# A Mamba-2 and attention trunk on one core: weight-pair stores queued behind the next loads, and the output projection in half-precision pairs from the second block on

## The chip, the cores and the metric

One core of one Trainium2 chip runs the whole program in one launch. The metric is the device time of that core in microseconds (us). The engines are PE (matrix products; PEld is its loading of the stationary operand), DVE (vector operations), ACT (scalar functions), POOL, and SP, which here only issues transfers. Each works through its own list of instructions in order and waits on signals of the others.

## The reference, cut to what matters

2048 tokens of width 1024 go through one Mamba-2 layer, then one attention layer, then a normalization. The change lies in the Mamba-2 layer alone:

```
proj = rms_norm(x) @ w_in              # z (2048), xBC (3072), dt (32 heads)
xBC  = silu(causal_conv4(xBC))         # xs (2048), B and C (4 groups x 128)
y    = scan over time of (x, dt, B, C) in chunks, plus D * x
y    = y * silu(z)                     # 4 groups of 512 channels
y    = y * rsqrt(mean(y*y over the group) + eps) * g_out
h    = x + y @ w_out                   # (2048 x 2048) @ (2048 x 1024)
```

All is float32, and the result has to keep more precision than a single product in half precision or in the fast float format (fp32r) gives.

## The kernel before

**Products.** Every large product is made of three (`mm3`, L86 to L88): each operand is a pair of a high part and the remainder (low part), and high x high, high x low and low x high are added up in PSUM. Pairs are either fp32r (`split`: ACT writes the high part, L109 or with a scale L112, DVE the low part, L110 or L113) or half-precision, f16 (`pair16`: ACT L117, DVE L118). f16 has little range, so values in f16 pairs are first multiplied by a power of two (`up`) that is worked out on the chip from a sum of squares (`powers`, with a PE product at L144 that adds over the partitions), and the result is multiplied by the inverse (`down`).

**Tiling.** The Mamba layer goes through 4 blocks b of 512 tokens, and in each through 4 groups g of channels: 16 items (b, g). For each item `ssd(b, g)` runs over 4 chunks c of 128 tokens. Between its steps a loop places pieces of the other work: the output product `outp` of the item before, and the input products `xbc` and `zgate` of the item behind; in the timeline these are what PE does between the short steps of `ssd`. In block 0 the loop also places `scan(g)`, which reads the weights of a later group of w_in and sums their squares (ACT L180) to find the power. A framework schedules: it writes each engine's list from the program's order, with priorities (`high_priority(AHEAD)`, 10 steps, for making and loading weights) and from buffers that come free. Weight pairs live in `wsp` (6 buffers), raw weights in `wraw` (3).

**Weights.** In block 0 `wpair` loads raw weights of w_in, makes an f16 pair of two k steps (L117, L118) and stores it to DRAM (`wi_d`, L209); later blocks load that pair (L211). For the output product, block 0 loads w_out, multiplies it by g_out and makes an fp32r pair (`wunit`, L130, L112, L113), and stores its two halves (`wo_d`, L511, 64 stores of 256 KB). Blocks 1 to 3 load each pair back (L506, 96 loads of 512 KB).

**The end of a chunk in `ssd`.** y is multiplied by the gate and `down` on DVE (L678). ACT sums its squares into `ms` (L680). PE transposes y in four pieces (L683), ACT and DVE make an fp32r pair of it (L685, tile yT), and `outp` uses it as the stationary operand against wsp (group `mm<-wsp,yT` in the profile). The factor 1/rms per token (`rr`, L690) is applied when the product is added to the residual hs (L519). The list of DVE also holds, for the next chunk, the differences L634 on the tile big, which comes by a transfer from cumT (L622); ACT then takes the exponential (L635) and DVE multiplies (L636).

**The start.** Before the first item the power of w_in's group 0 is found in two scans: kind 0 (B and C), then kinds 1 and 2 together (xs and z): four squares of tiles hs and four of tiles yT on ACT, L144 on PE, the powers on DVE, and with them the first weight pairs. Then `steps(0)` makes the step sizes (L533 on PE, 16 products, and L573), and `xbc(0,0)`, `zgate(0,0)` run together with the scan of group 1 (tiles hx).

## Time and profile before

| | |
|---|---|
| median of 3 runs | 3200.43 us (3199.44 to 3203.22) |
| the profiled execution | 3204.34 us, span 3202.6 us |
| granted clock of PE | 0.995 |
| busy PE, DVE, ACT | 96%, 75%, 60% of the span |
| start (before the first item's work) | 0 to 80 us |
| block 0 (with the making of weights) | 80 to 480 us |
| blocks 1 to 3 | 480 to 1460 us, then to 1650 with the start of attention between |
| attention | 1650 to 3202 us |

A row of the timeline has the start in us, the length in us, the engine, the line, what is written and read (tiles by the program's names, then shape and type), and in square brackets how long the engine had been idle and what released it. A row of grouped waits has the engine and line that waited, what for, the total in us, the times and the longest. Lengths of PE products overlap, so the pace is read from start to start.

### The profile page before, as it was taken

What the parts mean: (1) busy time and instruction counts of PE and PEld (TensorE: products, weight loads), DVE (VectorE), ACT (ScalarE), POOL (GpSimd) and SP (SyncE); (2) the same over time, 40 slices, a digit from 0 to 9 for tenths busy, and PEclk for the clock granted to TensorE, in tenths of its full rate; (3) what the DMA queues carried; (4) which work ended last, traced back from release to release, by engine and by line L of the source; (5) the groups of instructions that cost most, each with busy time, mean ns of one, the idle gap of its engine ahead of it and who ended that gap; (6) DMA issues with size and microseconds to landing.
All of it is one profiled execution on the core that took longest, in us unless ns stands there. A gap on an engine that the chain in (4) does not pass through costs nothing.

```text
span 3202.6 us, 51345 instructions
## 1 busy us (share of the span) xinstructions
PE 3085.4 (96%) x17744; PEld 2163.4 (68%) x17744; DVE 2401.2 (75%) x5178; ACT 1914.1 (60%) x4817; POOL 609.1 (19%) x842
## 2 busy tenths in 40 slices
PE   6999999999999999999999999999999999999998
PEld 3455555666655566665878888877777777777777
DVE  7778887767677676767876665678888888888675
ACT  8667554444455444455645554477877778778522
POOL 0212122121122212212111211322212122222100
PEclk9999999999999999999999999999999999999999
DMA  8667645334443345334476656853444434443485
GB/s 285 229 214 230 229 144 194 127 126 145 141 157 130 115 151 189 127 128 142 141 271 218 225 190 194 265 111 78 95 81 84 81 78 96 79 97 99 101 270 159
DMA packets 207113, 497.61 MB, mean 155 GB/s; under 512 B 27746, under 2 KB 51042, under 8 KB 205412
## 3 DMA queue, kind: packets, MB, share of 16 engines
q1 hardware_dynamic: 165444, 370.04, 35.6%
q0 software_dynamic: 41408, 124.29, 15.9%
q8 instruction: 140, 2.29, 0.3%
q14 instruction: 121, 0.99, 0.1%
HBM read 362.22 MB, written 131.99 MB: 154 GB/s over the span
## 4 chain that ended last, share of the span: by engine, by line
PE 64%; DVE 13%; ACT 8%; DMA 8%; issue 6%; POOL 1%; SPq 0%; ACTq 0%; DVEq 0%; POOLq 0%
PE mm L86 13%; PE mm L87 12%; PE mm L88 12%; PE tr L1044 6%; PE tr L87 3%; PE tr L1054 3%; PE tr L1055 3%; PE tr L86 3%; PE tr L88 3%; DVE cacc L460 3%; DMA big<-cumT 2%; DMA wraw<-in_ssm_w_in_dram 1%; DVE big L634 1%; ACT Pr L1029 1%; PE tr L656 1%
## 5 line engine op out<-in xcount | busy, mean ns | idle before, releaser
L118 DVE SCALAR_TENSOR_TENSOR PTs<-tr,PTs 128x512 f16<-128x512 f32 (+3 forms) x640 | 374.9, 607 | 93.9 <-ACT PTs L117 86.8
L117 ACT ACTIVATE PTs<-tr 128x512 f16<-128x512 f32 (+3 forms) x640 | 328.5, 541 | 141.4 <-PE tr L1044 140.3
L1017 DVE TENSOR_REDUCE mx<-mm 128x1 f32<-128x512 f32 (+2 forms) x631 | 375.7, 608 | 45.7 <-PE mm L88 42.6
L1029 ACT ACTIVATE Pr<-mm,nm 128x512 f32<-128x512 f32 (+2 forms) x631 | 395.7, 636 | 23.1 <-DVE nm L1021 21.4
L1044 PE MATMUL tr<-pack,Pr 128*128 128x128 f32 x2176 | 317.6, 273 | 1.0 <-ACT Os L1061 0.9
L86 PE MATMUL mm<-K,xT 96*128 96x512 f32 (+2 forms) x639 | 288.2, 451 | 23.3 <-ACT Pr L1029 21.8
L86 PE MATMUL mm<-xT,wsp 128*128 128x512 f16 (+1 forms) x800 | 304.9, 381 | 0.3 <-DVE sz L484 0.3
L88 PE MATMUL mm<-xT,wsp 128*128 128x512 f16 (+1 forms) x800 | 303.4, 380 | 1.4 <-DVE wsp L118 1.3
L87 PE MATMUL mm<-xT,wsp 128*128 128x512 f16 (+1 forms) x800 | 303.7, 380 | 0.0
L1044 PEld LDWEIGHTS tr<-pack,Pr 128*128 128x128 f32 x2176 | 253.5, 141 | 49.7 <-ACT Os L1061 1.7
L648 ACT ACTIVATE Xw<-tr,d_wend 128x64 f32<-128x64 f32 x512 | 183.4, 359 | 133.3 <-DVE Xd L644 133.3
L460 DVE SCALAR_TENSOR_TENSOR cacc<-craw,pack,cacc 128x512 f32<-128x512 f32 x288 | 213.6, 764 | 30.5 <-ACT cacc L458 28.9
L86 PE MATMUL mm<-wsp,xT 128*128 128x512 f16 (+1 forms) x640 | 232.4, 363 | 1.6 <-ACT craw L454 1.6
L88 PE MATMUL mm<-K,xT 96*128 96x512 f32 (+2 forms) x639 | 231.6, 362 | 0.0
L87 PE MATMUL mm<-wsp,xT 128*128 128x512 f16 (+1 forms) x640 | 231.6, 362 | 0.0
L87 PE MATMUL mm<-K,xT 96*128 96x512 f32 (+2 forms) x639 | 231.4, 362 | 0.0
L88 PE MATMUL mm<-wsp,xT 128*128 128x512 f16 (+1 forms) x640 | 231.1, 362 | 0.0
L1054 PE MATMUL tr<-PTs,xT 128*128 128x512 f16 (+3 forms) x640 | 222.0, 348 | 0.1
L86 PE MATMUL mm<-wsp,yT 128*128 128x512 f32 x512 | 208.1, 409 | 13.3 <-DVE sz L484 4.7
L1055 PE MATMUL tr<-PTs,xT 128*128 128x512 f16 (+3 forms) x640 | 219.4, 347 | 0.0
L606 POOL TENSOR_TENSOR Xp<-Xw,Xp 128x512 fp32r<-128x512 f32 x64 | 81.8, 1278 | 711.3 <-ACT Xp L605 382.4
L88 PE MATMUL mm<-wsp,yT 128*128 128x512 f32 x512 | 203.0, 397 | 1.4 <-DVE yT L110 1.4
(411 smaller groups left out, 7418.2 us busy)
## 6 DMA issues: line engine op xcount, KB each, us to landing
wsp<-wi_d SPq DMA_DIRECT2D x96, 512.0 KB, 3.7
wsp<-wo_d SPq DMA_DIRECT2D x96, 512.0 KB, 3.5
big<-cumT SPq DMA_DIRECT2D x64, 512.0 KB, 4.9
wi_d<-wsp SPq DMA_DIRECT2D x32, 512.0 KB, 3.4
wo_d<-wsp SPq DMA_DIRECT2D x64, 256.0 KB, 2.5
xT<-qn_d POOLq DMA_DIRECT2D x64, 256.0 KB, 4.4
K<-kn_d POOLq DMA_DIRECT2D x15, 1024.0 KB, 9.2
hx<-in_ssm_w_in_dram SPq DMA_DIRECT2D x48, 256.0 KB, 4.3
```

The source lines that it names most:

```text
L86: mm(out, l_hi, r_hi, start=start, stop=False)
L87: mm(out, l_hi, r_lo, start=False, stop=False)
L88: mm(out, l_lo, r_hi, start=False, stop=stop)
L117: self.nc.scalar.activation(hi, src, AF.Copy, scale=scale)
L118: self.nc.vector.scalar_tensor_tensor(lo, src, scale, hi, ALU.mult, ALU.subtract)
L460: nc.vector.scalar_tensor_tensor(acc, raw[:, k:k + TB], wk[k], acc, ALU.mult, ALU.add)
L648: act(Xw[:, hc], px[:, hc], AF.Copy, scale=wend[:, h0 + h:h0 + h + 1])
L1017: v.tensor_reduce(mx[:, n:n + 1], s[:, :w], AX.X, ALU.max)
L1029: nc.scalar.activation(x[:, :w], s[:, :w], AF.Exp, bias=nm, accum_out=sm[:, n:n + 1])
L1044: nc.tensor.transpose(pt[:, j * P:(j + 1) * P], st["P"][j][kb], self.ident)
L1054: nc.tensor.matmul(st["O"][:, c], vals[h][:, kb, :], u[:, 0], start=kb == 0, stop=False)
L1055: nc.tensor.matmul(st["O"][:, c], vals[h][:, kb, :], u[:, 1], start=False, stop=kb == nk - 1)
```

## The change

It has three parts.

1. *Stores of pairs.* `wpair` first issues the loads of both raw tiles of a pair and then converts them; the store of the pair goes into a list `owed` and is issued (`settle`) behind the loads of the next pair.
2. *The start.* The scan of kinds 1 and 2 is two scans: kind 1 before `steps(0)`, kind 2 together with `xbc(0,0)`; the scan of group 1 runs together with `zgate(0,0)` alone.
3. *The output product.* Block 0 works as before, but stores nothing; ACT takes the sum of squares of each of the 32 weight tiles besides. At the end of block 0 a power of two for w_out is worked out (`out_power`). Block 1 loads the raw tiles again, makes f16 pairs of two k steps (the gain is g_out times the power) and stores them, 16 stores of 512 KB. Blocks 2 and 3 load one such pair of 512 KB for two k steps. From block 1 on, y is brought to f16's range per token: three DVE operations on one column turn the sum of squares into a power of two (L740 to L742), ACT multiplies y by it (L743), and then y is transposed (L745) and made into an f16 pair. The inverse power goes into `rr`.

```
+    def settle(self):
+        for d, u in self.owed:
+            self.nc.sync.dma_start(d, u)
+        self.owed = []
...
             if b == 0:
+                raws = []
                 for j in range(2):
...
+                    raws.append(raw)
+                self.settle()
+                for j, raw in enumerate(raws):
                     self.pair16(u[:, j, 0], u[:, j, 1], raw, self.up[:, g, kind:kind + 1])
-                nc.sync.dma_start(d, u)
+                self.owed.append((d, u))
             else:
+                self.settle()
                 nc.sync.dma_start(u, d)
...
-        rest = self.scan(0, (1, 2), lambda kind: first.pop(0), True)
+        rest = [self.scan(0, (kind,), lambda kind: first.pop(0), True) for kind in (1, 2)]
...
-        for part in (hold, self.prep(0, self.g0), rest, self.steps(0), together(self.xbc(0, 0), ahead),
+        for part in (hold, self.prep(0, self.g0), rest[0], self.steps(0), together(self.xbc(0, 0), rest[1]),
                      together(self.zgate(0, 0), ahead)):
...
+    def w_out(self, b, g, n, j, made):
...
+        with self.tc.high_priority(AHEAD):
+            if b == 0:
+                raw, u = self.raw(False), self.t(self.wp, "wsp", [P, 2, TB], F32R, bufs=WSP)
+                load(raw, j)
+                self.settle()
+                self.split(u[:, 0], u[:, 1], raw, gain(self.go, j))
+                at = 8 * g + 4 * n + j
+                nc.scalar.activation(self.t(self.sp, "yt", [P, D], BF16, bufs=2)[:, :TB], raw, AF.Square,
+                                     scale=gain(self.go, j), accum_out=self.wss[:, at:at + 1])
+                return u[:, 0], u[:, 1]
+            u, d = self.t(self.wp, "wsp", [P, 2, 2, TB], F16, bufs=WSP), self.wo_d[g, n, j // 2]
+            if b == 1:
+                raws = [self.raw(False) for _ in range(2)]
+                for i in range(2):
+                    load(raws[i], j + i)
+                self.settle()
+                for i in range(2):
+                    self.pair16(u[:, i, 0], u[:, i, 1], raws[i], gain(self.gou, j + i))
+                self.owed.append((d, u))
+            else:
+                self.settle()
+                nc.sync.dma_start(u, d)
+        made[j + 1] = u[:, 1, 0], u[:, 1, 1]
+        return u[:, 0, 0], u[:, 0, 1]
+
+    def out_power(self):
...
+        v.tensor_reduce(ss, self.wss, AX.X, ALU.add)
+        self.powers(ss, 1, up, self.wod)
+        v.tensor_scalar(self.gou, self.go, up, None, ALU.mult)
...
     def outp(self, b, g):
...
-                if b:
-                    with self.tc.high_priority(AHEAD):
-                        u = self.t(self.wp, "wsp", [P, 2, TB], F32R, bufs=WSP)
-                        nc.sync.dma_start(u.bitcast(F32), d)
-                    return [u[:, i, :] for i in range(2)]
-                w = self.wunit(a["ssm_w_out"][r0:r0 + P, n * 512:(n + 1) * 512], 512,
-                               self.go[:, 4 * g + j:4 * g + j + 1])
-                for i in range(2):
-                    nc.sync.dma_start(d[:, i], w[i].bitcast(F32))
-                return w
+                return self.w_out(b, g, n, j, made)
...
     def ssd(self, b, g):
...
             act(junk, y, AF.Square, scale=0.5 * 512.0 ** -0.5, accum_out=ms[:, c:c + 1])
+            if b:
+                e = self.t(self.sm, "pwe", [P, 1], I32)
+                v.tensor_scalar(e, ms[:, c:c + 1].bitcast(I32), 24, None, ALU.logical_shift_right)
+                v.tensor_scalar(e, e, -1, 127 + 63 + 8, ALU.mult, ALU.add)
+                v.tensor_scalar(pw[:, c:c + 1].bitcast(I32), e, 23, None, ALU.logical_shift_left)
+                act(y, y, AF.Copy, scale=pw[:, c:c + 1])
...
-            u = self.t(self.sp, "yT", [P, 2, 4, P], F32R, bufs=4)
-            self.split(u[:, 0], u[:, 1], ps.rearrange("p (j t) -> p j t", j=4))
+            u = self.t(self.sp, "yT", [P, 2, 4, P], F16 if b else F32R, bufs=4)
+            (self.pair16 if b else self.split)(u[:, 0], u[:, 1], ps.rearrange("p (j t) -> p j t", j=4))
...
-        v.tensor_scalar(rr, r, 0.5, None, ALU.mult)
+        if b:
+            v.tensor_scalar(pw.bitcast(I32), pw.bitcast(I32), -1, 0x7F000000, ALU.mult, ALU.add)
+            v.scalar_tensor_tensor(rr, r, self.wod, pw, ALU.mult, ALU.mult)
+        else:
+            v.tensor_scalar(rr, r, 0.5, None, ALU.mult)
```

Since the framework writes the lists, these are the places at which they differ most. In the new program the lines have moved: L678 is L734, L680 is L736, L683 is L745, L674 is L730, L673 is L729, L634 is L690, L605 is L661, L460 is L473, L622 is L678, L206 is L213, L519 is L572, L533 is L588; L196 is the store in `settle`, L511 the raw load of w_out.

The list of SP, block 0, where the first output product's weights are made; wraw are raw weights, wsp pairs, wi_d and wo_d the places in DRAM. Before:

```order
L206 DMA wraw_1577<-in_ssm_w_in_dram 128x512
L622 DMA big_1659<-cumT_424 128x1024
L209 DMA wi_d<-wsp_1510 128x2048
L130 DMA wraw_1842<-in_ssm_w_out_dram 128x512
L209 DMA wi_d<-wsp_1572 128x2048
L130 DMA wraw_1852<-in_ssm_w_out_dram 128x512
L130 DMA wraw_1901<-in_ssm_w_out_dram 128x512
L511 DMA wo_d<-wsp_1844 128x512
L511 DMA wo_d<-wsp_1854 128x512
L511 DMA wo_d<-wsp_1844 128x512
L130 DMA wraw_1911<-in_ssm_w_out_dram 128x512
```

The same place now:

```order
L213 DMA wraw_1593<-in_ssm_w_in_dram 128x512
L196 DMA wi_d<-wsp_1528 128x2048
L511 DMA wraw_1860<-in_ssm_w_out_dram 128x512
L511 DMA wraw_1871<-in_ssm_w_out_dram 128x512
L196 DMA wi_d<-wsp_1590 128x2048
L678 DMA big_1889<-cumT_409 128x1024
L175 DMA hx_1705<-in_ssm_w_in_dram 128x512 x2
L511 DMA wraw_1921<-in_ssm_w_out_dram 128x512
```

The stores of w_out pairs are gone from between the raw loads; stores of w_in pairs (wi_d) stand where they stood, one pair behind the loads.

The list of DVE behind y in the second chunk of item (1,1); st is the state, cacc the convolution. Before:

```order
L678 SCALAR_TENSOR_TENSOR y_6277<-y_6277,down,sz_5936 128x512
L674 TENSOR_TENSOR st_373_2063<-st_373_2063,tr_6344 128x512
L634 TENSOR_SCALAR big_6678<-big_6678,d_cum_4090 128x128 x7
L673 TENSOR_TENSOR st_373_2063<-st_373_2063,d_dec_4092 128x512
L634 TENSOR_SCALAR big_6678<-big_6678,d_cum_4090 128x128
L110 TENSOR_TENSOR yT_6387<-tr_6382,yT_6387 128x512
```

The same place now:

```order
L734 SCALAR_TENSOR_TENSOR y_6369<-y_6369,down,sz_5992 128x512
L730 TENSOR_TENSOR st_388_2083<-st_388_2083,tr_6436 128x512
L690 TENSOR_SCALAR big_6780<-big_6780,d_cum_4110 128x128
L740 TENSOR_SCALAR pwe_6475<-ms_6089 128x1
L690 TENSOR_SCALAR big_6780<-big_6780,d_cum_4110 128x128
L741 TENSOR_SCALAR pwe_6475<-pwe_6475 128x1
L690 TENSOR_SCALAR big_6780<-big_6780,d_cum_4110 128x128
L742 TENSOR_SCALAR pw_6090<-pwe_6475 128x1
```

The three operations of the power (pwe, pw) stand among the differences L690, the first of which comes ahead of them and needs the tile big from its transfer.

The list of ACT at the start: yt is a scratch tile, hs and yT hold raw weights of kinds 1 and 2. Before:

```order
L180 ACTIVATE yt_322,ss_307<-hs_210 128x1024
L180 ACTIVATE yt_327,ss_307<-yT_211 128x1024
L180 ACTIVATE yt_331,ss_307<-yT_212 128x1024
L180 ACTIVATE yt_335,ss_307<-yT_213 128x1024
L180 ACTIVATE yt_339,ss_307<-yT_214 128x1024
L117 ACTIVATE wsp_428<-big_205,up 128x256
L117 ACTIVATE wsp_461<-big_205,up 128x256 x2
```

The same place now:

```order
L180 ACTIVATE yt_325,ss_310<-hs_213 128x1024
L117 ACTIVATE wsp_413<-big_208,up 128x256
L117 ACTIVATE wsp_439<-big_208,up 128x256 x2
L117 ACTIVATE wsp_465<-big_209,up 128x256 x2
L117 ACTIVATE wsp_499<-big_209,up 128x256 x2
L117 ACTIVATE wsp_545<-hs_210,up 128x512 x2
L592 ACTIVATE yt_360<-tr_342,dtdown 64x512
L180 ACTIVATE yt_427,ss_424<-yT_214 128x1024
```

The squares of kind 2 (yT) have moved behind the weight pairs of B, C and the first of xs, and behind the step sizes.

More of the change, by code (lines that the diff above doesn't have):

```diff
@@ L280, in layer_constants @@
         self.xdown = cp.tile([P, 1], F32, name="xdown")
+        self.wss, self.gou = (cp.tile([P, n], F32, name=m) for m, n in (("wss", 32), ("gou", 16)))
+        self.wod = cp.tile([P, 1], F32, name="wod")
         self.dtdown = cp.tile([P, 1], F32, name="dtdown")
@@ L488, in zgate, with load, gain @@
         self.sz[b, g] = out
+    def w_out(self, b, g, n, j, made):
+        if j in made:
+            return made.pop(j)
+        nc = self.nc
+        def load(raw, j):
+            r0 = g * 512 + j * P
+            nc.sync.dma_start(raw, self.a["ssm_w_out"][r0:r0 + P, n * 512:(n + 1) * 512])
+        def gain(x, j):
+            return x[:, 4 * g + j:4 * g + j + 1]
+        with self.tc.high_priority(AHEAD):
[23 more added lines that the diff above has]
+    def out_power(self):
+        v = self.nc.vector
+        ss = self.t(self.sm, "ss", [P, 3, 4], bufs=2)[:, 0, 0:1]
+        v.tensor_reduce(ss, self.wss, AX.X, ALU.add)
+        up = self.t(self.sm, "up0", [P, 2], bufs=1)[:, 0:1]
+        self.powers(ss, 1, up, self.wod)
+        v.tensor_scalar(self.gou, self.go, up, None, ALU.mult)
+        v.tensor_scalar(self.wod, self.wod, 0.5, None, ALU.mult)
     def outp(self, b, g):
@@ L522, in outp @@
         if g == G - 1:
+            if b == 0:
+                self.out_power()
             for i in range(4):
@@ L595, in ssd @@
         ms = self.t(self.sm, "ms", [P, 4])
+        pw = self.t(self.sm, "pw", [P, 4])
         self.yT[b, g] = []
@@ L1246, in run @@
             self.wi_d = [dp.tile([G, KD // 2, P, 2, 2, n], F16, name=f"wi{i}_d") for i, n in enumerate((256, 512, 512))]
-            self.wo_d = dp.tile([G, 2, 4, P, 2, TB], F32, name="wo_d")
+            self.wo_d = dp.tile([G, 2, 2, P, 2, 2, TB], F16, name="wo_d")
             self.xq = whole.enter_context(tc.tile_pool(name="xq", bufs=8, side="right"))
```

4 lines of the change are left out of this document (2 added, 2 removed).

## The prediction

> **What bounds the kernel now.** I read the page's busy times first, then a table of five stretches of the span, and only then single rows of the stretches that the change touches.
>
> ```profile
> PE 3085.4 (96%) x17744; PEld 2163.4 (68%) x17744; DVE 2401.2 (75%) x5178; ACT 1914.1 (60%) x4817; POOL 609.1 (19%) x842
> 0.00:80.00 80.00, 54.73 (x254) 28.75 (x255) 57.62 (x182) 64.70 (x124) 5.61 (x20) 0.96 0.88 284
> 80.00:480.00 400.00, 374.46 (x2171) 217.17 (x2170) 326.04 (x669) 261.04 (x631) 74.03 (x90) 0.98 0.64 209
> 480.00:1460.00 980.00, 967.48 (x5713) 584.66 (x5712) 700.81 (x1422) 476.90 (x1288) 202.53 (x250) 1.00 0.43 144
> 1460.00:1650.00 190.00, 178.12 (x1049) 136.90 (x1047) 140.88 (x296) 107.02 (x265) 37.06 (x45) 1.00 0.52 171
> 1650.00:3202.50 1552.50, 1510.63 (x8565) 1195.97 (x8564) 1175.81 (x2612) 1004.39 (x2511) 289.90 (x437) 1.00 0.53 140
> ```
>
> In a row of stretches stand its limits, its length, then busy us and instructions of PE, PEld, DVE, ACT and POOL, the clock, the DMA share and GB/s. PE is busy 96% of the span, so time goes only where PE's own work shrinks or one of its few idle stretches closes. The change ends with the Mamba part, near 1650 us; the 1552 us behind it (attention) run the same instructions and I count nothing there. Blocks 1 to 3 (480 to 1460) leave PE idle for 12.5 us of 980: there, a shorter matmul is worth nearly its full size, and any new wait of PE costs nearly its full size. Block 0 (80 to 480) leaves 25.5 us idle, the start 25 us, the end of the Mamba part 12 us. So I go through four places: the output matmuls of blocks 1 to 3, the new step in front of the transposes of y, the start, and block 0 with what moves from it into block 1.
>
> **1. Half-precision output matmuls, blocks 1 to 3.** Two rows of a run of them in float pairs, 22 intervals apart, and two rows of the input projection, whose operands are half-precision, 5 apart:
>
> ```profile
> 855.33 0.40 PE L87 MATMUL mm<-wsp,yT 128*128 128x512 f32 x1
> 860.36 0.39 PE L88 MATMUL mm<-wsp,yT 128*128 128x512 f32 x1
> 903.98 0.38 PE L86 MATMUL mm<-xT,wsp 128*128 128x512 f16 x1
> 905.06 0.38 PE L88 MATMUL mm<-xT,wsp 128*128 128x512 f16 x1
> L86 PE MATMUL mm<-wsp,yT 128*128 128x512 f32 x512 | 208.1, 409 | 13.3 <-DVE sz L484 4.7
> ```
>
> Start to start that is 5.03/22 = 228.6 ns against 1.08/5 = 216 ns, for the same 128x512 product. The durations overlap, so the intervals count. Of each of the three lines 512 run in four blocks, 384 in blocks 1 to 3: 1152 matmuls x 12.6 ns = 14.5 us. Bounds: 13 us if a tenth of them wait for something else anyway; 23 us if the durations (0.40 against 0.38) told the gain rather than the intervals. I take 15. The Trainium skill, TensorE: Matmul & The Clock Gate, section "Wait — 56ns, not 53.3ns?", gives 215.7 ns for 512 columns without a word on the type; the half-precision rows agree, the float rows do not, and by that rule this term would be nothing.
>
> **2. The step between y and its transposes.** In blocks 1 to 3 each of 48 chunks gets three tiny dependent DVE operations and an ACT copy over 128x512 before the four transposes. A second chunk of an item:
>
> ```profile
> 885.18 0.83 DVE L678 SCALAR_TENSOR_TENSOR y<-y,down,sz 128x512 f32<-128x512 f32 x1
> 885.94 0.67 DVE L674 TENSOR_TENSOR st<-st,tr 128x512 f32<-128x512 f32 x1
> 886.11 0.63 ACT L680 ACTIVATE yt<-y 128x512 f32<-128x512 f32 x1 [2.71 <-DVE y L678]
> 886.65 0.19 ACT L680 ACTIVATION_READ_ACCUMULATOR yt<-y 128x1 f32 x1
> 886.74 0.61 ACT L605 ACTIVATE Sp<-st 128x512 fp32r<-128x512 f32 x1
> 887.56 1.22 DVE L634 TENSOR_SCALAR big<-big,d_cum 128x128 f32<-128x128 f32 x1 [0.95 <-DMA big<-cumT]
> 887.83 0.38 PE L683 MATMUL tr<-pack,y 128*128 128x128 f32 x2
> 904.78 0.83 DVE L678 SCALAR_TENSOR_TENSOR y<-y,down,sz 128x512 f32<-128x512 f32 x1
> 911.17 0.60 PE L683 MATMUL tr<-pack,y 128*128 128x128 f32 x4
> 932.70 0.74 DVE L678 SCALAR_TENSOR_TENSOR y<-y,down,sz 128x512 f32<-128x512 f32 x1
> 936.52 0.60 PE L683 MATMUL tr<-pack,y 128*128 128x128 f32 x4
> 936.18 0.15 DVE L226 TENSOR_TENSOR rss<-rsy 128x4 f32<-128x4 f32 x1
> 936.37 0.16 DVE L228 SCALAR_TENSOR_TENSOR rsq<-rsx,rss 128x4 f32<-128x4 f32 x1
> ```
>
> Today PE comes to the transposes by its own order: y is ready at 886.01, the transposes start at 887.83, 1.8 us later, without a wait. In the third chunk of the item the slack is 5.6 us (905.61 to 911.17), in the first no less, in the fourth 3.1 (933.44 to 936.52). With the new step: sum of squares in hand at 886.84; three DVE steps of 0.19 to 0.2 us (the spacing of the tiny rows at 936) to about 887.5; copy of 0.63 (the Square's own size) to about 888.2. That is 0.4 us later than PE now comes. In the first and third chunks matmuls cover the step; in the fourth it takes 2.2 to 3.2 against 3.1, because the order puts rsqrt steps of the same item between the tiny ones. The order also moves 1 to 10 matmuls ahead of the transposes where slack was smallest, which is free work in the gap. What could be dearer is a chunk like the one at 887.56: there the order puts L690 (today's L634) ahead of the tiny ones, and that waits for a DMA:
>
> ```profile
> DVE big L634 <- DMA big<-cumT: 29.2, 25, 1.9
> ```
>
> 29.2 us in 25 waits from 480 to 1460, 1.2 us each. Eight of the nine second chunks of groups 1 to 3 have an L690 in front; if half of them wait that long, it is some 5 us. Bounds: +1 us (only the three second chunks of group 0, 0.4 each) and +10 us (nine at 1.0, a bit in the fourth chunks). I take +4. The 48 copies are 48 x 0.63 = 30 us more on ACT, 477 of 980 us busy there: off the path but for the above.
>
> **3. The start.** Kind 1's squares alone now release the first scales; kind 2's four follow later.
>
> ```profile
> 26.90 1.05 ACT L180 ACTIVATE yt<-yT 128x1024 bf16<-128x1024 f32 x1
> 30.02 1.05 ACT L180 ACTIVATE yt<-yT 128x1024 bf16<-128x1024 f32 x1
> 31.49 0.56 PE L144 MATMUL tr<-ss,ones 128*128 128x2 f32 x2 [6.99 <-DVE ss L185]
> 31.98 5.38 PE L533 MATMUL tr<-xT,wdt 128*64 128x512 f16 x16
> 50.82 0.46 PE L573 MATMUL tr<-big,pack 128*128 128x128 f32 x2 [2.06 <-DVE big L571]
> ```
>
> Four squares, 26.90 to 31.05, stand between PE's last product and L144: 4.15 us, so the PE idle of 6.99 falls to about 2.8. Not all stays. The squares come back behind the step-size matmuls, ahead of weight pairs that PE then needs, and the wait for the step-size chain (2.06 at 50.82) grows, since PE reaches it sooner while DVE's chain starts only some 4 us sooner too. I count half of one square chain back, 0.7 us: -3.5. Ends: -6 (everything stays, and the 16 products in 5.38 us, 336 ns each, run nearer to 216) and +1 (the squares push the first pairs of group 1 by their whole 4.15 and one more). The Trainium skill, same page, section "The two states you'll see", lets the clock fall after an idle window of about 3.4 us; 6.99 is over it and 2.8 under, and by it those 16 would save another 1.9 us.
>
> **4. Block 0, and what goes to block 1.** Removed in block 0: 64 stores of 256 KB. Added: 32 ACT squares. The queue that carries the stores:
>
> ```profile
> SPq L511 <- ACT wsp L112: 58.1, 22, 9.5
> SPq L511 <- DVE wsp L113: 20.3, 17, 4.6
> 157.60:198.60 41.00, 33.96 (x186) 25.93 (x185) 32.18 (x90) 30.66 (x79) 5.54 (x5) 0.88 0.77 239
> 563.40:589.60 26.20, 26.20 (x148) 21.26 (x147) 15.53 (x29) 8.12 (x25) 3.04 (x3) 1.00 0.37 121
> L117 ACT ACTIVATE wsp<-wraw,up x48: 492/711/836, 186.9 to 348.3; 128x512 f16<-128x512 f32 x32, 128x256 f16<-128x256 f32 x16
> L118 DVE SCALAR_TENSOR_TENSOR wsp<-wraw,up,wsp x48: 469/741/1753, 187.5 to 352.5; 128x512 f16<-128x512 f32 x32, 128x256 f16<-128x256 f32 x16
> ```
>
> The store lines hold SP 78 us in 39 waits, and loads of weights, of cumT and of the scan stand behind them. In the stretch 157.6 to 198.6, where the first output product runs, PE is idle for 7 us, where a stretch of the same sort in block 1 (563.4) has none. Against it: 32 x (0.63 + 0.19) = 26 us more on ACT, the engine that now has 30.66 of 41 us busy in that stretch and makes the very pairs PE waits for; spread over four items, some 3 us in each of the halves where PE already waits. I take -3 for the stores against the squares, with ends of -12 (half of the 25.5 us idle of block 0) and +8 (a third of the 26). The reordered pair stores of the input projection I cost at nothing: in SP's list loads and stores of the pairs come in the order they already had.
>
> Block 1 takes over 16 conversions of two tiles each: 32 x 0.71 on ACT, 32 x 0.74 on DVE, 24 us more on DVE in some 250 us, of which it is busy 72% (700.81 of 980). Loads fall from 32 x 512 KB to 64 x 256 KB raw halves, half the bytes. What hides it are the 10 steps by which weights are made ahead; where the cover fails, an output product waits for a conversion of 1.5 us a pair. 0 to +8; I take +3.
>
> **5. Blocks 2 and 3 and the end.** One load of 512 KB now brings two weights. Inside the blocks these loads are hidden. At the last output product they are not:
>
> ```profile
> 1607.86 2.43 SPq L506 DMA_DIRECT2D wsp<-wo_d  x2
> 1613.60 0.50 PE L86 MATMUL mm<-wsp,yT 128*128 128x512 f32 x1 [2.03 <-DMA wsp<-wo_d]
> 1617.50 0.51 PE L86 MATMUL mm<-wsp,yT 128*128 128x512 f32 x1 [1.54 <-DMA wsp<-wo_d]
> ```
>
> 3.6 us of waits; the second, at least, falls away with its load. -2.5 (0 to -4).
>
> **Sum:** -15 + 4 - 3.5 - 3 + 3 - 2.5 = -17 us. The profiled execution took 3204.3, 3.9 above the median of 3200.4 of the runs; from the median, 3183.4, rounded to 3184.
>
> **Rivals.** A measurement of this kernel tells 0.2%, 6.4 us, from no change.
> - *No faster matmul.* If the interval of the float products comes from the sequence they stand in and not from their type, term 1 is 0 and the sum -2: 3198. For it speaks only the rule quoted in part 1; against it, hundreds of both kinds run side by side in the same clock.
> - *Slower: the power waits behind cumT.* DVE works in order, so in each chunk where an L690 ahead of the tiny ones waits for its cumT, the power, the copy and the transposes are late by it. At 1.2 us (the mean of the 25 waits) less the margin, plus a transpose chain that then delays the split and the next output product, all 48 chunks would lose 0.8 us: 38 us in place of 4, and 3184 + 34 = 3218. It decides from 0.44 us a chunk (21 us, which brings the sum to 0). Against: first and third chunks have over 5 us of slack, which leaves 24 chunks at 0.9.
> - *Conversions are not hidden.* ACT in block 0 and DVE in block 1 at their upper ends, +8 each: sum -17 + 11 + 5 = -1, 3199. For it: ACT already holds SP up for 58 us there.
> - *The stores were the cause of block 0's idle.* At -12 the sum is -26: 3174; with the start's -6 it is 3172.
>
> **Chances.** Forecast 0.62; no faster matmul 0.05 (same); the power waits 0.11 (half of it same, half slower); conversions 0.12 (0.09 same, 0.03 slower); stores 0.10 (faster). Faster 0.72, same 0.20, slower 0.08. The range reaches from the store rival with a little more, 3169, to the rivals that end near no change, 3199; the forecast's own range is 3175 to 3192.
>
> **What would show it.** Right: output products at 216 ns; PE's wait before L144 about 2.8 us; blocks 1 to 3 shorter by some 4 us each; waits of PE for ACT's y copy (L743) in second chunks, a few tenths each; no L506 waits near 1613. Wrong: such waits of over 1 us in many chunks, PE waiting for w_out conversions in block 1, or a longer stretch around the first two output products of block 0.

## The result: slower, and the profile after

The changed kernel takes 3219.92 us (median of 4 runs, 3216.31 to 3225.75) against 3201.17 us: the ratio is 1.0047, 95% interval 1.0034 to 1.0061, some 15 to 19 us slower where 17 us faster was forecast. The profiled execution has a span of 3217.6 us. Its busy times, and four of the five stretches cut where they were cut before (limits, length, busy us and instructions of PE, PEld, DVE, ACT, POOL, clock, DMA share, GB/s):

```profile
PE 3074.8 (96%) x17748; PEld 2059.0 (64%) x17748; DVE 2433.8 (76%) x5386; ACT 1986.8 (62%) x4961; POOL 609.3 (19%) x842
0.00:80.00 80.00, 59.44 (x283) 30.97 (x284) 56.58 (x179) 63.11 (x119) 6.59 (x21) 1.00 0.90 300
80.00:480.00 400.00, 361.84 (x2098) 208.86 (x2097) 321.76 (x667) 276.05 (x680) 72.89 (x89) 0.97 0.50 163
480.00:1460.00 980.00, 947.15 (x5670) 493.05 (x5668) 724.71 (x1584) 525.56 (x1368) 195.99 (x243) 1.00 0.38 129
1460.00:1650.00 190.00, 178.48 (x1065) 118.36 (x1064) 146.64 (x332) 111.02 (x273) 41.79 (x47) 1.00 0.44 141
```

PE's work did shrink, by 10.6 us over the span. Its idle time grew by more: from 25.5 to 38 us in 80 to 480, from 12.5 to 33 us in 480 to 1460. DMA carries less in both. So the change removed what it meant to remove, and PE waits for something new.

Stretches of equal limits hold different work once a kernel is late, so the runs below are read by milestones: the start of y's first transpose in the last chunk of an item, each a row of PE's timeline. Differences to the kernel before, in us, stretch by stretch:

| kernel | block 0, to item (0,3) | block 1 | block 2 | block 3, items (3,0), (3,1) | items (3,2), (3,3) | behind them |
|---|---|---|---|---|---|---|
| before, milestone at | 468.9 | 845.8 | 1221.6 | 1400.6 | 1565.5 | 3202.6 |
| changed | +10.6 | +8.3 | +0.8 | +0.1 | +8.9 | -13.5 |
| no squares | -1.7 | +6.4 | +1.0 | -0.6 | +8.8 | -10.9 |
| no power per token | +10.5 | +3.4 | -3.3 | -2.5 | -2.8 | -2.8 |
| neither | -3.0 | +2.4 | -4.8 | -2.0 | -2.6 | -3.2 |
| neither, sample of squares | -0.3 | +2.8 | -4.8 | -2.4 | -2.7 | -4.1 |
| the same, no conversions | +1.9 | -5.5 | -3.7 | -2.1 | -2.7 | -3.6 |

They come from one profiled execution each. The last column, with attention in it, varies by some us between executions of equal work, the middle ones by 1 to 2. Up to items (3,0), (3,1) PE does the same work between two milestones in the changed kernel as before, within two instructions of its count. In items (3,2), (3,3) it does 1016 instructions where the kernel before does 962: the 54 more come from behind the milestone (some 12 us at 216 ns each, an estimate), so the last two columns are to be read as one sum. Block 0's column varies as well: over the nine kernels below in which block 0 does the same work (a sample of squares in place of all) it lies between -2.6 and +6.4. The +9.1 to +10.6 of the four kernels with squares of the raw tile stand outside that; the -3.0 to +2.2 of the others don't tell them apart.

The faster products are there. Two rows of a run of them, 21 intervals apart, 4.53/21 = 215.7 ns:

```profile
873.92 0.38 PE L86 MATMUL mm<-wsp,yT 128*128 128x512 f16 x1
878.45 0.38 PE L86 MATMUL mm<-wsp,yT 128*128 128x512 f16 x1
```

The new wait is in the groups of what PE waited for (total us, times, longest), from 480 to 1680:

```profile
PE tr L745 <- ACT y L743: 19.7, 23, 2.0
PE tr L712 <- DVE big L692: 6.7, 6, 1.7
PE tr L87 <- POOL Xp L662: 6.1, 13, 0.7
```

In the kernel before, over the same stretch, the largest group and the group of the transposes of y are:

```profile
PE tr L656 <- DVE big L636: 4.5, 7, 1.6
PE tr L683 <- DVE y L678: 1.3, 3, 0.7
```

Here is one of the new waits, in the second chunk of item (1,1), in the rows of DVE, POOL, ACT and PE:

```profile
612.00 0.83 DVE L734 SCALAR_TENSOR_TENSOR y<-y,down,sz 128x512 f32<-128x512 f32 x1
612.75 0.67 DVE L730 TENSOR_TENSOR st<-st,tr 128x512 f32<-128x512 f32 x1
613.99 0.29 DVE L690 TENSOR_SCALAR big<-big,d_cum 128x128 f32<-128x128 f32 x1 [0.57 <-DMA big<-cumT]
614.20 0.15 DVE L740 TENSOR_SCALAR pwe<-ms 128x1 int32<-128x1 int32 x1
614.26 1.33 DVE L690 TENSOR_SCALAR big<-big,d_cum 128x128 f32<-128x128 f32 x1
615.51 0.14 DVE L741 TENSOR_SCALAR pwe<-pwe 128x1 int32<-128x1 int32 x1
615.77 0.14 DVE L742 TENSOR_SCALAR pw<-pwe 128x1 int32<-128x1 int32 x1
...
614.24 1.26 POOL L662 TENSOR_TENSOR Sp<-st,Sp 128x512 fp32r<-128x512 f32 x1 [1.96 <-ACT Sp L661]
...
616.00 0.72 ACT L743 ACTIVATE y<-y,pw 128x512 f32<-128x512 f32 x1 [1.84 <-DVE pw L742]
...
616.78 0.66 PE L745 MATMUL tr<-pack,y 128*128 128x128 f32 x4 [1.76 <-ACT y L743]
```

The sum of squares was in hand at 613.6. The first tiny operation stands behind an L690 that waits for its tile until 613.99, the second behind another that takes 1.33 us instead of 0.2 to 0.3, while POOL is at work on Sp (1.26 us). PE stands still for 1.76 us.

In block 0, SP's rows around item (0,2), and what PE then waits for:

```profile
275.61 5.53 SPq L422 DMA_DIRECT2D hx<-in_x_dram  x4
286.92 0.33 SPq L678 DMA_DIRECT2D big<-cumT  x1
287.34 8.71 SPq L511 DMA_DIRECT2D wraw<-in_ssm_w_out_dram  x5
...
291.82 0.80 PE L86 MATMUL tr<-Xp,Bt 128*128 128x512 f32 x1 [4.93 <-ACT Xp L661]
```

Five of the eight loads of w_out for this item are issued from 287.34 on, behind the four loads of block 1's x; the kernel before had issued six of them by 266, these two last:

```profile
264.92 1.16 SPq L130 DMA_DIRECT2D wraw<-in_ssm_w_out_dram  x2
```

The changed kernel is 9 us late from here on: the first transposes of item (0,2) come at 309.0 against 299.7, where those before them, in the last chunk of (0,1), were 2.5 us late. What PE waits for in the row at 291.82 is ACT. Between 286.40 and 289.69 ACT does three of the new squares (2.7 us) ahead of Xp; so this row does not show PE waiting for the late loads themselves.

### The profile page after: what moved, and what is told of

The parts are those of the page before. It is cut to its first block, busy times and chain, and to the rows that moved or that the text cites. A ratio compares the mean times of both kernels' runs of the same rounds, so it can differ in the third digit from the quotient of the medians.

```text
span 3217.6 us, 51583 instructions
## 1 busy us (share of the span) xinstructions
PE 3074.8 (96%) x17748; PEld 2059.0 (64%) x17748; DVE 2433.8 (76%) x5386; ACT 1986.8 (62%) x4961; POOL 609.3 (19%) x842
## 4 chain that ended last, share of the span: by engine, by line
PE 42%; DMA 3%; ACT 3%; DVE 2%; issue 1%; SPq 0%; POOL 0%; ACTq 0%; DVEq 0%
PE mm L86 7%; PE mm L88 6%; PE mm L87 6%; PE tr L1110 6%; PE tr L1120 3%; PE tr L1121 3%; PE tr L87 3%; PE tr L88 3%; PE tr L86 3%; ACT Pr L1095 1%; DMA os<-ri_d 1%; DVE PTs L118 1%; DMA wraw<-in_mla_w_in_dram 1%; ACT PTs L117 1%; PE mm L1082 1%
## 5 line engine op out<-in xcount | busy, mean ns | idle before, releaser
L473 DVE SCALAR_TENSOR_TENSOR cacc<-craw,pack,cacc 128x512 f32<-128x512 f32 x288 | 215.2, 768 | 27.7 <-ACT cacc L471 26.6
L662 POOL TENSOR_TENSOR Xp<-Xw,Xp 128x512 fp32r<-128x512 f32 x64 | 82.7, 1291 | 720.5 <-ACT Xp L661 446.6
L86 PE MATMUL mm<-wsp,yT 128*128 128x512 f16 (+1 forms) x512 | 197.5, 391 | 6.3 <-DVE sz L497 2.1
L87 PE MATMUL mm<-wsp,yT 128*128 128x512 f16 (+1 forms) x512 | 197.7, 386 | 1.2 <-DVE wsp L113 1.2
```

The costliest lines, as they stand in the source:

```text
L86: mm(out, l_hi, r_hi, start=start, stop=False)
L87: mm(out, l_hi, r_lo, start=False, stop=False)
L473: nc.vector.scalar_tensor_tensor(acc, raw[:, k:k + TB], wk[k], acc, ALU.mult, ALU.add)
```

## The experiments

Ratios are to the kernel before, of runs on the same chip, with 95% intervals; a ratio of 0.001 is 3.2 us.

**Squares, and where they read.** The first kernel replaces the sum by a constant, the second squares the high part in place of the raw tile (the code of all experiments is shortened here):

```
-                nc.scalar.activation(yt, raw, AF.Square, scale=gain(self.go, j), accum_out=self.wss[:, at:at + 1])
+        nc.gpsimd.memset(self.wss, 16.0)                                                       # first
+                nc.scalar.activation(yt, u[:, 0].bitcast(F32), AF.Square, accum_out=...)        # second
```

> The changed kernel without the 32 squares of w_out tiles in block 0 (the sum is a constant, 16 per column, in their place). Theory H (the squares read the raw tiles and hold the three wraw buffers, so in the lists the w_out loads of the third item of block 0 land behind the loads of block 1's x, and PE waits for them; 7 us are lost at that item, 4 us more later in block 0): 3207 us, 11 to 14 less than the changed kernel, and the first chunk of item (0,2) no longer late. Theory Q (the 26 us of ACT time are the cost, wherever the lists put the loads): also about 3207, so it is told from H by the next kernel. Rival S (block 0 lost its time to the split start or the removed stores): 3218 to 3221.

> The changed kernel with the same 32 squares of the same length on ACT, but taken of the high part in wsp instead of the raw tile, so that the raw tile is free as soon as the pair is made; SP's list then has all eight w_out loads of item (0,2) ahead of block 1's x loads. Theory H: nearly as fast as without squares, 3208 to 3212. Theory Q: no gain, 3217 to 3221.

Measured: 0.9996 (0.9986 to 1.0005) and 1.0019 (1.0010 to 1.0028). Of the changed kernel's 1.0047 the squares are 0.0051, 16 us; 9 us of them go when only the read is moved off the raw tile, the other 7 when ACT's work goes too (by the ratios; block 0's milestones, +2.2 and -1.7, are too near to each other to show the 7). So theory H holds for the larger part, and theory Q may hold for the rest. The second kernel is 2.0 us late at the last chunk of item (0,1) and 2.1 at the first of (0,2), where the changed one went from 2.5 to 9.3: the step is gone. Its rows of SP show w_out ahead of x again:

```profile
267.40 3.78 SPq L511 DMA_DIRECT2D wraw<-in_ssm_w_out_dram  x3
271.27 0.38 SPq L678 DMA_DIRECT2D big<-cumT  x1
273.43 0.81 SPq L175 DMA_DIRECT2D hx<-in_ssm_w_in_dram  x2
275.08 3.44 SPq L422 DMA_DIRECT2D hx<-in_x_dram  x3
```

The experiment shows that it matters which tile the squares read. That the loads' place behind x is the way from there to the 9 us is read from these lists; the lists of ACT and PE moved too, and no run moved the loads alone.

**The power per token.** The third kernel leaves out L740 to L743 and takes a constant scale for y (and its inverse, a constant too, in `rr`); the fourth keeps them and puts the other work's step between the copy and the transposes:

```
-            if b:                                        # third: no power, no copy
-                e = ...; act(y, y, AF.Copy, scale=pw[:, c:c + 1])
+            self.pair16(u[:, 0], u[:, 1], ps, 2.0 ** -8)
...
                 act(y, y, AF.Copy, scale=pw[:, c:c + 1])
+                yield                                    # fourth: the step boundary from behind the pair to here
```

> The changed kernel without the power of two per token: the three DVE operations and the ACT copy of y are left out, y is brought to half precision by one constant, 2 to the -8. All else stays, the half-precision products too. Theory W (the transposes of y wait for the copy, 19.7 us in 23 waits, and the next chunk's chain is late by it; that took the 14 us of the faster products): 3220 - 20 = 3200 us, 3196 to 3204. Rival M (the products' gain itself was eaten elsewhere, by the weights' conversions in block 1 or by the tile big): 3212 to 3220.

> The changed kernel with one step boundary moved: from block 1 on the piece of other work that stood behind y's transposes now stands ahead of them, so PE has 18 to 24 more input products to do while the power and the copy are made. All work of the change is kept. Theory W: the waits for the copy go, 3199 to 3205 us. If the 19.7 us only hide waits that stood there anyway (for the tile big, for Xp), these take their place: 3212 to 3220.

Measured: 1.0001 (0.9992 to 1.0011), as theory W had it, 15 us less than the changed kernel; and 1.0067 (1.0051 to 1.0082), slower still, outside what either reading of that run allowed. What PE waits for in the fourth kernel from 480 to 1680:

```profile
PE tr L712 <- DVE big L692: 11.5, 8, 3.0
PE tr L628 <- DVE big L626: 10.5, 2, 5.4
PE tr L87 <- POOL Xp L662: 8.8, 11, 0.9
PE tr L258 <- DVE st L730: 5.3, 2, 3.2
PE tr L746 <- ACT y L743: 2.3, 3, 1.7
```

The wait for the copy is all but gone (2.3 us), and others stand there: the step sizes of the next block (L628, over 5 us each time), the tile big of the next chunk. By my reading the products that now cover the copy were the cover of those; no run shows it. By milestones the loss is in block 1: +15.5 (with 12 of PE's instructions more in it) against +8.3 in the changed kernel.

**Both out, and a sample of squares.** The fifth kernel joins the first and the third. The sixth keeps a power that comes from the weights: the first of each four tiles is squared (8 of 32, of the high part, scale 2 to count four times).

```
+                if j == 0:
+                    at = 2 * g + n
+                    nc.scalar.activation(yt, u[:, 0].bitcast(F32), AF.Square, scale=2.0, accum_out=self.wss[:, at:at + 1])
```

> The changed kernel with both suspected costs out: no squares in block 0 (a constant sum) and no power per token (one constant, 2 to the -8). What stays is the split start, the removed stores, the conversions in block 1 and the half-precision products. If the two costs are separate (16 us and 15 us in the runs before), they add up: 19 - 16 - 15 = -12 us against the kernel before, ratio 0.996. If they hide each other (block 0's lateness and the transposes' waits share PE's idle time), less: 0.999 to 1.000. The forecast's sum without these two terms was -17, ratio 0.9947.

> As the run without either cost, but with a power for w_out that still comes from the weights: 8 of the 32 tiles are squared (the first of each four, of the high part, times 4). Eight squares of 0.8 us are 6.5 us of ACT; if ACT time counts at the rate that the squares of the high part showed (7 us for 26), 2 us over the run without: ratio 0.9965 to 0.997. If any square in that place does harm (by the order of the lists), 5 us or more over it.

Measured: 0.9955 (0.9943 to 0.9967) and 0.9961 (0.9948 to 0.9974); medians 3191.1 and 3192.7 us. The two costs add up (0.0047 - 0.0051 - 0.0046 = -0.0050 expected, -0.0045 seen). Both kernels beat the one before and the changed one. They leave out the range that the power per token gives to y.

**The start.** The split start alone in the kernel before, and the old start in the changed kernel:

```
-        rest = self.scan(0, (1, 2), ...)   ->   rest = [self.scan(0, (kind,), ...) for kind in (1, 2)]
```

> The kernel before with the split start alone. Theory D (PE starts 6 us earlier, but in item (0,0) weights come no faster than the transfers bring them, so the gain is gone one chunk later): 0 to -1 us, ratio 0.9995 to 1.0000. The forecast's term: -3.5, ratio 0.9989. If the split harms the later scans' order in block 0: ratio over 1.0005.

> The changed kernel with the start of the kernel before. Theory D: the same as the changed kernel within 1 us, ratio 1.0045 to 1.005. If the split start was the part that made block 0 late: under 1.003. If the split start brings what the forecast said: 1.0058.

Measured: 1.0003 (0.9995 to 1.0012) and 1.0047 (1.0035 to 1.0059): theory D within the intervals; a gain of the forecast's 3.5 us lies outside the first of them. A loss of 2 us or more (over 1.0005) is not excluded. At the first product behind the start PE is early, as forecast:

```profile
28.40 0.35 PE L144 MATMUL tr<-ss,ones 128*128 128x1 f32 x2 [2.84 <-DVE ss L185]
28.69 3.64 PE L588 MATMUL tr<-xT,wdt 128*64 128x512 f16 x16
49.26 0.46 PE L628 MATMUL tr<-big,pack 128*128 128x128 f32 x2 [0.77 <-DVE big L626]
```

The idle time of 6.99 us is 2.84, the 16 products take 3.64 us for 5.38, and the wait at the step sizes has become shorter, 0.77 for 2.06. In the changed kernel the first transposes come 6.3 us early (100.0 for 106.3), the second chunk's 0.2 us late (131.1 for 130.9); in the kernel with the split start alone 5.7 us early, then 3.0 early, then 0.6 late.

**What of the power costs.** A base with the sample of squares and the full power; then only the three tiny operations; only the copy, of a constant; and the power in two operations.

```
     e9:  DVE, DVE, DVE, ACT copy by pw        e10: DVE, DVE, DVE, no copy
     e11: no DVE, ACT copy by a constant       e12: both shifts in one DVE operation, then mult and add, then the copy
```

> The changed kernel with the sample of 8 squares, and with the power of two per token as the change has it: the base for the next three. From the two costs as measured (16 less 1.5 us of the squares gone, 15 of the power still there): ratio 0.9998 to 1.0005.

> The same with the three tiny DVE operations per chunk, whose result nothing uses, and without the ACT copy; y goes to half precision by the constant. Theory W (the cost is that the transposes depend on a chain through DVE's list and ACT): nearly all of the 15 us gone, ratio 0.996 to 0.997. Rival L (the cost is the load: 29 us of DVE time more in blocks 1 to 3, that delays the tiles big): half or more stays, 0.998 to 1.000.

> The same with the ACT copy, but of a constant column in place of the power, and without the three DVE operations: the copy follows the square at once (0.09 + 0.63 + 0.19 + 0.63 = 1.5 us behind y, under the 1.8 us that PE takes to come). Theory W: ratio 0.996 to 0.9975, waits for the copy under 5 us. Rival A (ACT's 30 us more are the cost): 0.999 to 1.000.

> The base with the power made in two DVE operations (both shifts in one) rather than three; all else is kept, the copy too. Theory W with the queue on DVE (the operations stand among L690, which wait for cumT): each of some 22 waits shorter by 0.2 us or more, 3 to 6 us under the base. If the waits are set by the arrival of cumT alone: the same as the base within 1 us.

Measured: 1.0019 (1.0009 to 1.0028), 0.9977 (0.9968 to 0.9986), 1.0000 (0.9991 to 1.0008), 1.0024 (1.0014 to 1.0035). Against the 0.9961 without either (taken on another chip, six runs), the full power is 18.6 us, the tiny operations alone 5 us, the copy alone 12.5 us, each within about 5 us.

The base itself missed its expectation: with a quarter of the squares it is no faster than the second kernel with all of them (1.0019 both). So the 7 us that the squares' work on ACT seemed to cost are not firm: here three quarters of it went without a gain, while on another chip the same sample cost 2 us over no squares (sixth against fifth). By pairs of kernels the power is 13 us (first against fifth), 15 (changed against third) or 18.6.

The tiny operations alone lie between the two theories. My expectation for the copy alone failed: it follows the square at once, waits for nothing on DVE, and still costs two thirds; the number is that of rival A, ACT's load. Part of it stands in PE's waits for the copy:

```profile
PE tr L743 <- ACT y L741: 6.0, 8, 1.7
```

Eight waits. Six stand in chunks where PE used to come to the transposes 0.15 to 1.0 us behind y: the first chunks of (1,3) and (2,3), the third of (3,2), the first three of (3,3). The other two are the second chunks of (1,2) and (2,2), where it used to come 1.5 us behind. Its last two items are 4.3 us late, where without a copy they are 2.7 us early (some 3.5 us of that, an estimate, is work of PE from behind the milestone: 978 instructions for 962). The other 6.5 us of the 12.5 are not in waits for the copy, and what they are is open. The two-operation form won nothing (e12 against e9: +0.0005, intervals overlap), though its waits for the copy, from 480 to 1680, are shorter (first the three operations, then the two):

```profile
PE tr L746 <- ACT y L744: 16.2, 22, 2.0
```

```profile
PE tr L745 <- ACT y L743: 14.1, 20, 1.7
```

Why that didn't shorten the whole is not settled. In the one execution of each, the stretches from block 1 to items (3,0), (3,1) are 2.7 us shorter in sum, but block 0, with the same work, is 2.4 us longer, and what lies behind (3,1) is 3.3 us longer.

**Where the power costs, and the conversions.** The power in some chunks alone, the constant in the others. And, in the kernel without power, pairs of w_in that lie ready in DRAM in place of w_out's: this kernel leaves w_out out of blocks 1 to 3, its output is not the layer's, and it serves for the time alone.

```
+            on = b and (c % 2 == 0 and (b, g) < (3, 2))      # e13; e14: c % 2 == 1; e15: (b, g) >= (3, 2) alone
...
-                    load(raws[i], j + i) ... self.pair16(...) ... self.owed.append((d, u))
+            nc.sync.dma_start(u, self.wi_d[1][g, 2 * n + j // 2])                                  # e16
```

> As the base with a sample of squares, but with the power per token only in the first and third chunks of the items of blocks 1 to 3, the last two items excepted (20 of 48 chunks); elsewhere y takes the constant 2 to the -8. By the forecast these are covered by matmuls: ratio 0.9961 to 0.9970, at most 3 us over the run without any power (0.9961), and that from the first chunks of the groups 3. Rival (load on DVE and ACT counts wherever it is): 20/48 of the 18 us, 0.9985.

> The power only in the second and fourth chunks of the same items (20 of 48 chunks). If the second chunks' waits (1 to 2 us each by the trace, in the groups 1 to 3) are the cost of blocks 1 to 3: 10 to 13 us over the run without, ratio 0.9992 to 1.0002. By load alone: 0.9985. By the forecast's term (+4): 0.9973.

> The power only in the eight chunks of the last two items, where y's transposes today follow y at once. By the milestones the Mamba part ends 9 to 11 us later there, but the work that PE does meanwhile is missing behind it, and 8 us come back: 2 to 5 us over the run without, ratio 0.9967 to 0.9977. If nothing comes back: 0.9990 to 0.9995.

> The run without any power per token and with the sample of squares, but blocks 1 to 3 load pairs of w_in that lie in DRAM already, in place of w_out's: no raw loads, no conversions and no stores in block 1, and the output of the products is not that of the reference. If block 1's missing gain is the conversions: block 1 gains 3 to 4 us as block 2 does, 5 to 8 us under the run without power, ratio 0.9936 to 0.9945. If not: the same as that run, 0.9961, within 1.5 us.

Measured: 0.9988 (0.9979 to 0.9997), 0.9995 (0.9987 to 1.0004), 0.9977 (0.9968 to 0.9986) and 0.9943 (0.9929 to 0.9956). Over the 0.9961: first and third chunks 8.6 us, second and fourth 10.9, last two items 5.1. They add up to 25 where all together cost 18.6; each has an interval of about 5 us and all three share that of the 0.9961, so the shares are rough. Second and fourth chunks cost the 10 to 13 us that was expected, though the waits for the copy in that execution are only 7.8 us in sum. First and third were to be free, at most 3 us; that failed, and the number is that of the rival by which the load counts wherever it is (0.9985). The steps from one chunk's transposes to the next speak against that rival: in groups 0 and 1 of block 2 those of the first and third chunks carry the same load and differ from those of the kernel without power by at most 0.4 us. The third chunk of group 2 there is 2.9 us longer than in the kernel before, with a wait of PE of 1.2 us for the copy, and the first chunk of group 3 is 2.7 us longer than without the power; part of it comes back in the chunks behind. In block 1 the third chunk of (1,2) is 5.7 us longer and the next gives it back; 2.3 and 2.7 us in the fourth chunks of (1,0) and (1,1), which have no power here, are not explained.

In the last items the Mamba part ends 11.6 us later than without the power (+8.9 against -2.7), and 7.6 us come back behind it: 54 of PE's instructions have moved from behind to ahead of that milestone. The conversions, with block 1's raw loads and stores that go with them, are 5.8 us by time, which is about as large as its interval, and 8.3 us in block 1's milestones (-5.5 against +2.8).

## Why the prediction was wrong, point by point

**Right: the products.** 12.6 ns each was forecast, 15 us in all. The pace is 215.7 ns for 228.6. Block 2, where the kernels without power differ from the one before only in these products and their loads, gains 3.3 to 4.8 us in the table; 384 x 12.6 ns are 4.8. The rival *no faster matmul* falls, and with it the reading that the type plays no part in the figure of 215.7 ns that the Trainium skill gives (TensorE: Matmul & The Clock Gate, section "Wait — 56ns, not 53.3ns?"): half-precision products meet it, the float pairs of the kernel before did not.

**Failed: "I take -3 for the stores against the squares".** Block 0 was +10.6 us at its last milestone and -1.7 without the squares. I priced the squares by ACT's time in the stretch where PE already waits, and that part (at most 7 us, and not firm) lay inside my range of -12 to +8. The dearer part, 9 us, is not ACT time as such, for it goes when the same squares read the other tile. A square that reads the raw tile holds one of the three wraw buffers, the framework then lists the w_out loads later, and they fall behind loads of x that themselves wait for buffers (4.3 us in four waits from 250 to 320); that this is the path to PE is the likely reading, not shown by a run of its own. The text counted 78 us of SP waits as something that goes with the stores, and did not ask what the loads would stand behind instead, although the order of SP's list was to be read. Most of block 0's lateness arises at item (0,2), the stretch of the second output product, which is one of the signs of being wrong that the prediction named. What the removed stores bring by themselves is not told: block 0 is at -3.0 in the kernel without squares and power and at -2.0 in the one with the new start alone, too near to each other for a price.

**Failed: "I take +4" for the step between y and its transposes.** It costs 13 to 18.6 us, by the pairs above. The mechanism of the rival *the power waits behind cumT* was there, as the chunk at 612 shows, but alone it stays under the 21 us from which that rival was to decide. Its 3218 lies next to the measured 3220 by luck: it gave the power 38 us, and what it had too much is about what the squares cost.

Three things were mis-sized. I read the slack from the four chunks of one item, (2,0), and let it stand for all: in the first chunks of (1,3) and (2,3) and in the last six chunks of all, PE used to come only 0.15 to 1.0 us behind y, less than the copy's 0.72 us and the three tiny operations together. The 1 to 10 products that the order moved into the gap I called free, but they are missing later, as the 54 of the last two columns are. Second, I gave half of the eight second chunks a wait of 1.2 us. There are 23 waits of 19.7 us in all; of the second chunks those of (1,1) and (2,1) wait longest, 1.8 us each.

Third, I took 0.2 us for each step of the power, as if the tiny operations stood side by side in DVE's list. In the third chunk of (2,2) the sum of squares is in hand at 1112.4. Four convolution operations (L473, 3.74 us) stand ahead of the first tiny operation, at 1116.15, and the third comes at 1118.25; PE waits 1.23 us for the copy, although it used to come there 6.1 us behind y. So the slack of over 5 us in the third chunks, which the prediction held against this rival, did not cover it there. The slow L690 could be seen beforehand too: the prediction shows one of 1.22 us, at 887.56, in front of where the tiny ones were to stand. The rows of before could have shown the slack as well: at each of the 48 chunks it is a subtraction of two rows.

**Failed: "-3.5" for the start.** The mechanism was right to a few tenths: idle 2.84 us for "about 2.8", and the 16 products ran in 3.64 us, near what the Trainium skill, TensorE: Matmul & The Clock Gate, section "What's actually happening" ("The two states you'll see"), would give when the idle stays under its window; the granted clock of 0 to 80 us is 1.00 where it was 0.96. The wait for the step sizes, which was to grow, became shorter. But being early is worth nothing: one to two chunks later PE is where it was. The time is 1.0003 (0.9995 to 1.0012): at most 1.6 us gained. That the next item waits for its weights' transfers I expected in theory D; the runs show that the gain goes, not by which transfer.

**Too small: "+3" for the conversions.** 5.8 us by time, inside the 0 to +8 that was given, and with 8.3 us by milestones at its end. Without them block 1 gains 5.5 us; with them, and no power, it is 2.4 to 3.4 us longer than before. The working has "64 x 256 KB" for block 1's raw loads; they are 32 (64 is the count of blocks 0 and 1), and half the bytes holds for 32. Block 1 is 377 us long where it has "some 250", and 3183.4 would have rounded to 3183; the forecast does not turn on these.

**About right: the end, -2.5.** The two waits for w_out pairs near the end are one of 0.53:

```profile
1632.53 0.38 PE L86 MATMUL mm<-wsp,yT 128*128 128x512 f16 x1 [0.53 <-DMA wsp<-wo_d]
```

That is 3.6 us of waits less 0.5. The reordered stores of w_in pairs were not tried by themselves; they stand in all kernels from the first to the sixth, the fastest of which is at 0.9955.

Put together with the measured sizes: products -14.5, power +15, squares +16, conversions +6, start 0, end -3 make +19.5; measured were +15 to +19. Power and squares were measured as differences to the changed kernel, so this is a check only in what is left: -14.5 + 6 - 3 = -11.5, where the fifth kernel, without both, measured -14.4 (0.9955, within 4 us). The forecast had every term of the change and the right sign for most; two of its six terms, both costs of new work in front of PE's waits, were out by some 11 and 19 us.

## What to carry to other kernels

Work that is added to an engine with time to spare is not free when another engine's next instruction depends on it: take the slack at every place where it is added, not at one, before calling it covered. An operation that only reads a buffer holds it, and in a kernel whose lists are written by a scheduler, that moves loads past others; ask of every new reader which buffer it keeps and what will queue ahead of the load that needs it. An early start is worth what the next limit lets through.

## What the runs showed of the hardware that I had not expected

A DVE operation can last until a POOL operation beside it ends. L690 over 128x128 is 0.2 to 0.3 us as a rule and took 1.33 us at 614.26, beside the 1.26 us of POOL's L662. Of the 512 L690 in the changed kernel, 25 took over 0.6 us, and each of these ends 0.08 to 0.09 us behind the end of an L662; none of the other 487 lies inside a POOL operation. The kernel before has 25 such L634 as well, one of them in the prediction's row at 887.56. In the last items even an operation of four columns does it, and the power that waits behind it is late:

```profile
1526.43 0.14 DVE L740 TENSOR_SCALAR pwe<-ms 128x1 int32<-128x1 int32 x1
1527.23 0.14 DVE L741 TENSOR_SCALAR pwe<-pwe 128x1 int32<-128x1 int32 x1
1527.30 1.16 DVE L232 TENSOR_SCALAR rsb<-rsx 128x4 int32<-128x4 int32 x1
1528.71 0.14 DVE L742 TENSOR_SCALAR pw<-pwe 128x1 int32<-128x1 int32 x1
...
1527.06 2.85 POOL L413 TENSOR_TENSOR wraw<-wraw,cacc 128x512 f32<-128x512 f32 x2 [5.15 <-DMA hx<-h_d]
...
1529.72 0.65 PE L745 MATMUL tr<-pack,y 128*128 128x128 f32 x4 [1.99 <-ACT y L743]
```

From the first tiny operation to the third it is 2.3 us here, where the working counted 0.4. The Trainium skill, GPSIMD Engine Reference, section "1. Specifications", says that POOL shares its SBUF interfaces with the vector engine and that DVE instructions in a two-port mode or with two SBUF inputs contend with it. The trace agrees in that the slow ones run beside POOL's and end with them; no run here shows in which mode they ran. The operations on one column were never slow: seven of the 144 lie inside a POOL operation, and none of them took over 0.16 us. That sharing is the cause was not tried by a run.
